# Slot and decay rows by bfloat16 products instead of float32 transposes, in a three-layer mixture-of-experts kernel

## The chip, the cores and the metric

One core of a Trainium2 chip runs the whole program in one launch. The metric is device time in microseconds. Before: median 1460.57 us of 3 runs (1457.16 to 1462.82).

## The reference

256 tokens with 1024 features pass through two layers of a first block and one layer of a second block. All inputs and outputs are float32.

- First block, per layer: a mixer (gated linear attention by chunks and a spatial gating unit), attention to a memory of 256 rows, and a mixture of 16 experts, each followed by a residual and a layer norm.
- Second block: a mixer with causal attention of 8 heads and a state space part (SSD) with 16 heads, a mixture of 16 experts, a gated projection and a last norm.
- Every mixture picks one group of four experts for a token, and two experts in it. An expert computes silu(x Wg) * (x Wu) and multiplies it by Wd; the token's result is the weighted sum over its two experts.
- In the SSD part the decay between tokens l and s of head h is exp(cs[l, h] - cs[s, h]) for s not after l, where cs is the cumulative sum of dt * a over the tokens:

```
decay_to_end = jnp.exp(da_cs[..., -1:] - da_cs)
y_diag = jnp.einsum('bgcls,bgjcls,bcsgjp->bclgjp', cb, decay_in, xdt)
```

## The kernel before

**Projections.** Weights come from HBM in pieces of 1 MB, in an order written out for SyncE's queue. A piece is split into a rounded part (ScalarE) and a rest (VectorE), the tiles `whl`, and three one-pass products stand for one exact one (`proj`, `proj_full`).

**Expert stages.** `moe` runs three times, once a layer. Tokens of an expert are put into 64 slots. `pos` (line 861) holds for each token (partition) and each of the 16 experts the slot, counted from 1, or 0. `Dm` is its one-hot form with tokens on partitions and gathers the tokens of four experts at a time into `XG` (`gather`). The loop at line 1011 takes the experts in eight pairs. For pair i TensorE does, in this order: gate product (`up(i, 0)`), spread of pair i-2 (`spread`), half a gather for the next four experts, up product (`up(i, 1)`), down product of pair i-1 (`down`), the other half gather, in pair 0 the slot gates (`slot_gates`), then `rows(i)`, a fill and `turned(i)`. The two experts of a pair fill 64 columns of the array each, so that their products run in pairs. `rows(i)` (line 969) makes `DT`, the one-hot form with slots on partitions and tokens along the row, by which `spread` brings results back to tokens: a column of `pos`, broadcast to 128 columns, is transposed by TensorE for each expert and each half of the tokens, so that each row of the result holds all tokens' slots; VectorE compares it with the slot's own number (`slot`).

All these TensorE instructions are pinned (`pin`, lines 66 to 75): they keep their order on the engine. Everything that is not pinned is ordered by a planner from modelled times and priorities. The weights of an expert are loaded into whatever buffer comes free (`expert_load`, line 206), in a fixed order; the first 20 pieces of a stage are loaded ahead of it, each later one waits until the products of an earlier piece are done.

**SSD.** `ssd` (line 1166) gets the cumulative sums `cs` from three products of a triangle matrix, then the masked products `cb` of the two groups, and then `heads(h0, n)` runs four heads at a time, between which stand the gate projections (`gates`, line 1317). A head needs its column of `cs` in every row: two transposes of the broadcast column (line 1201) into the PSUM tile `csr`; ScalarE or VectorE subtract the column and form `se`, ScalarE takes the exponential, VectorE multiplies by `dt` and `cb`, and three products (`ssy`) follow. `csr`, `dtp`, the gather's and the products' small PSUM tiles share four buffers (`rp`, line 59).

Of the kernel before, what the change touches and what calls it, by code (L numbers as in the profile page):

```python
# [9 lines left out]
BF16 = mybir.dt.bfloat16  # L10
AF = mybir.ActivationFunctionType
OP = mybir.AluOpType
# [3 lines left out]
T = 256  # L16
# [8 lines left out]
class Net:  # L25
# [94 lines left out]
    def setup1(self):  # L120
        nc, d = self.nc, self.jp
        self.upinc = self.const("upinc", [128, 128])
        self.ones = self.const("ones", [128, 128])
        self.later = self.const("later", [128, 128])
        self.half = self.const("half", [128, 2])
        self.iot = self.const("iot", [128, CAP])
        self.slot = self.const("slot", [128, 1])
        self.tri4 = self.const("tri4", [128, 4, 4])
        nc.vector.memset(self.ones, 1.0)
        self.upb = self.const("upb", [128, 128], BF16)  # L130
        self.ts(self.upb, d, 0.0, None, OP.is_gt)
        self.oneb = self.const("oneb", [128, 128], BF16)
        nc.vector.memset(self.oneb, 1.0)
        self.ts(self.upinc, d, 0.0, None, OP.is_ge)
        self.ts(self.later, d, 0.0, 1.0 / 16.0, OP.is_lt, OP.mult)
        nc.vector.memset(self.later[64:128, 0:64], 0.0)
        nc.vector.memset(self.half, 0.0)
        nc.vector.memset(self.half[0:64, 0:1], 1.0 / 16.0)
        nc.vector.memset(self.half[64:128, 1:2], 1.0 / 16.0)
        self.side = self.const("side", [128, 2])  # L140
        self.ts(self.side, self.half, 16.0, None, OP.mult)
        self.i2 = self.const("i2", [128, 64])
        self.add(self.i2, self.ident[:, 0:64], self.ident[:, 64:128])
        nc.gpsimd.iota(self.iot, pattern=[[1, CAP]], base=1, channel_multiplier=0,
                       allow_small_or_imprecise_dtypes=True)
        if self.cap < CAP:
            nc.vector.memset(self.iot[:, self.cap:], -1.0)
        scr = self.s2("scr", [128, 128])
        self.stt(scr[:, 0:64], self.i2, 1.0, self.iot, OP.mult, OP.mult, accum_out=self.slot)
        e = self.s2("e4", [128, 4, 4])  # L150
        nc.gpsimd.iota(e, pattern=[[-1, 4], [1, 4]], base=0, channel_multiplier=0,
                       allow_small_or_imprecise_dtypes=True)
        self.ts(self.tri4, e, 0.0, -1.0e-37, OP.is_lt, OP.mult)
# [694 lines left out]
    def moe(self, lg, xs, second, finish, gc, route, Wg, Wu, Wd, fill, source):  # L848


        nc = self.nc
# [9 lines left out]
        pos = self.sm("pos", [128, 2, 16], bufs=1)  # L861
        self.stt(pos, pp, 1.0, sel, OP.add, OP.mult)
        Dm = self.t8("Dm", [128, 2, 16, 64], F32R)

        def slots(e, n, tts=slice(0, 2)):
            m = tts.stop - tts.start
# [84 lines left out]
        H, DT, PS = {}, {}, {}  # L951
# [16 lines left out]

        def rows(i):
            with self.urgent("rows"):  # L970
                p = self.rp([128, 2, T], "dtp")
                for s in range(2):
                    for tt in range(2):
                        self.flip(p[:, s, tt * 128:(tt + 1) * 128],
                                  pos[:, tt, 2 * i + s:2 * i + s + 1].to_broadcast([128, 128]))
                DT[i] = self.s2("DT", [128, T], F32R)
                for s in range(2):
                    h = slice(64 * s, 64 * s + 64)
                    self.ts(DT[i][h], p[h, s], self.slot[h], None, OP.is_equal)

        def down(i, apart=False):

# [28 lines left out]
        for i in range(NE // 2):  # L1011
            pg = up(i, 0)
            if i > 1:
                spread(i - 2)
            gather(i // 2 * 4 + 4, (4 * (i % 2),))
            pu = up(i, 1)
            h = middle(pg, pu)
            if i:
                down(i - 1)
            gather(i // 2 * 4 + 4, (4 * (i % 2) + 2,))  # L1020
            if i == 0:
                slot_gates()
            if i == last and over:
                self.tc.keep_in_program_order(
                    nc.vector.tensor_scalar(flag, cm, float(self.cap), None, op0=OP.is_gt))
            rows(i)
            fill(i)
            turned(i, h)
# [137 lines left out]
    def ssd(self, xs, bc, zs, dt):  # L1166

        nc, a = self.nc, self.a
        da = self.sm("da", [128, 2, 16], bufs=1)
        self.stt(da, dt, -1.0, self.hv[:, 1:2, :].to_broadcast([128, 2, 16]), OP.mult, OP.mult)  # L1170
        p = self.rp([128, 2, 16], "csp")
        self.mm(p[:, 0, :], self.upinc, da[:, 0, :], True, True)
        self.mm(p[:, 1, :], self.ones, da[:, 0, :], True, False)
        self.mm(p[:, 1, :], self.upinc, da[:, 1, :], False, True)
        cs = self.sm("cs", [128, 2, 16], bufs=1)
        nc.vector.tensor_copy(cs, p)
        cb = []
        for g in range(2):
            p = self.rp([128, 384], "cbp")
            self.mm(p[:, 0:256], bc[:, g, 0:128], bc[:, 2 + g, :], True, True)  # L1180
            self.mm(p[:, 256:384], bc[:, g, 128:256], bc[:, 2 + g, 128:256], True, True)
            c = self.s2("cb", [128, 3, 128])
            p = p.rearrange("p (a b) -> p a b", a=3)
            self.mul(c[:, 0::2, :], p[:, 0::2, :], self.upinc[:, None, :].to_broadcast([128, 2, 128]))
            self.cp(c[:, 1, :], p[:, 1, :])
            cb.append(c.rearrange("p a b -> p (a b)"))
        u = self.t8("u")
        v = self.vec([a["ssd_norm_g_2"][0]])

        Y = []  # L1190

        def heads(h0, n):

            c = h0 // 8
            if h0 % 8 == 0:
                Y[:] = [self.acc([128, 8, 64], "ssy") for _ in range(2)]
            for h in range(h0, h0 + n):
                with self.urgent("sc"):
                    p = self.rp([128, 256], "csr")
                    for tt in range(2):  # L1200
                        nc.tensor.transpose(p[:, tt * 128:(tt + 1) * 128],
                                            cs[:, tt, h:h + 1].to_broadcast([128, 128]), self.ident)
                with self.urgent("se"):
                    e = self.s2("se", [128, 384])
                    for o, r, k in ((e[:, 0:256], p, cs[:, 0, h:h + 1]),
                                    (e[:, 256:384], p[:, 128:256], cs[:, 1, h:h + 1])):
                        if h % 2:
                            self.ts(o, r, k, 0.0, OP.subtract, OP.min)
                        else:
                            self.act(o, r, AF.Relu, scale=-1.0, bias=k)  # L1210
                    self.act(e, e, AF.Exp, scale=1.0 if h % 2 else -1.0)
                    self.stt(e[:, 0:256], e[:, 0:256], dt[:, 0, h:h + 1], cb[c][:, 0:256], OP.mult, OP.mult)
                    self.stt(e[:, 256:384], e[:, 256:384], dt[:, 1, h:h + 1], cb[c][:, 256:384], OP.mult, OP.mult)
                x0, x1 = (xs[:, i, h * 64:(h + 1) * 64] for i in range(2))
                with self.urgent("sy"):
                    self.mm(Y[0][:, h % 8, :], e[:, 0:128], x0, True, True)
                    self.mm(Y[1][:, h % 8, :], e[:, 128:256], x0, True, False)
                    self.mm(Y[1][:, h % 8, :], e[:, 256:384], x1, False, True)
            if (h0 + n) % 8:
                return  # L1220
            for tt in range(2):
                o = u[:, tt, c * 512:(c + 1) * 512]
                self.mul(o.rearrange("p (h d) -> p h d", h=8),
                         xs[:, tt, c * 512:(c + 1) * 512].rearrange("p (h d) -> p h d", h=8),
                         self.hv[:, 2, 8 * c:8 * c + 8, None].to_broadcast([128, 8, 64]))
                self.add(o, o, Y[tt].rearrange("p h d -> p (h d)"))
                self.mul(o, o, zs[:, tt, c * 512:(c + 1) * 512])
                ss = self.sm("ss", [128, 1])
                sq = self.s2("ssq", [128, 512])
                self.act(sq, o, AF.Square, accum_out=ss)  # L1230
                rs = self.sm("rs", [128, 1])
                self.rsqrt(rs, ss, 1e-6, 1.0 / 512.0)
                self.stt(o, o, rs, v[:, 0, c * 512:(c + 1) * 512], OP.mult, OP.mult)
        return u, heads
# [309 lines left out]
```

## Time and profile before

| | |
|---|---|
| median of 3 runs | 1460.57 us (1457.16 to 1462.82) |
| the profiled execution | 1460.11 us |
| its span | 1458.3 us |
| mean granted TensorE clock | 0.976 of full |
| HBM read | 419.18 MB |

The execution's own time is 1.8 us more than its span. Times in the trace are microseconds from the span's start. PE is TensorE's products, PEld its weight loads, DVE VectorE, ACT ScalarE. Products are pipelined, so that the duration of one is longer than the distance between two starts; float32 products appear as two instructions each, transposes as one. The DMA share is how much of the 16 DMA engines' time their packets fill.

### The profile page before, as it was taken

To read this page: it belongs to the slowest core of one execution; us is meant where nothing else is said; L and a number is where in the kernel's file an instruction comes from. 1 tells how busy PE (TensorE), PEld (TensorE's weight loads), DVE (VectorE), ACT (ScalarE), POOL (GpSimd) and SP (SyncE) were. 2 spreads that over 40 slices of the span, in tenths; PEclk is the share of its full clock that TensorE was granted. 3 is DMA by queue.
4 is the path that set the end of the run, shared out by engine and by line. 5 is a ranking of instruction groups with operands and counts; after the bars stand their busy time and mean duration, and the time that the engine had idled before them with its cause. 6 is when DMAs were issued, how large, how long until landed. Compare 5 with 4: busy or idle time off the path is not lost. (4 is left out here: it accounts for less than half of the span.)

```text
span 1458.3 us, 18050 instructions
## 1 busy us (share of the span) xinstructions
PE 1375.7 (94%) x7258; PEld 899.7 (62%) x7258; DVE 636.3 (44%) x1088; ACT 504.8 (35%) x784; POOL 63.7 (4%) x107
## 2 busy tenths in 40 slices
PE   8999999999988898999899998799999979999987
PEld 7889897444433686898444433499878864444335
DVE  5754754412111767654512111657776641212134
ACT  5634443211101474443211101548764440111132
POOL 2110000000000103000000000000000000000000
PEclk9999999999999999999899999899999989999998
DMA  9745557799999965446799999844534679999991
GB/s 341 271 173 173 174 178 267 280 399 421 420 419 420 320 224 175 145 174 243 297 404 380 422 420 420 326 133 134 185 129 137 227 288 378 421 380 420 420 380 44
DMA packets 101964, 421.50 MB, mean 289 GB/s; under 512 B 10676, under 2 KB 10896, under 8 KB 65008
## 3 DMA queue, kind: packets, MB, share of 16 engines
q1 hardware_dynamic: 97968, 409.17, 72.4%
q0 software_dynamic: 3904, 11.09, 2.3%
q8 instruction: 60, 0.98, 0.3%
q14 instruction: 32, 0.26, 0.0%
HBM read 419.18 MB, written 1.05 MB: 288 GB/s over the span
## 5 line engine op out<-in xcount | busy, mean ns | idle before, releaser
L64 PE MATMUL gu<-we,XG 128*64 128x512 f32 x1536 | 347.0, 596 | 4.2 <-DMA we<-in_w_up_dram 1.9
L78 DVE TENSOR_TENSOR whl<-raw,whl 128x1024 fp32r<-128x1024 f32 (+1 forms) x210 | 241.1, 1163 | 144.6 <-ACT whl L98 143.7
L98 ACT ACTIVATE whl<-raw 128x1024 fp32r<-128x1024 f32 (+1 forms) x210 | 208.2, 1009 | 200.8 <-PE acc L64 97.2
L64 PEld LDWEIGHTS gu<-we,XG 128*64 128x64 f32 x1536 | 108.1, 137 | 208.2 <-issue 193.9
L64 PE MATMUL acc<-whl,xTh 128*128 128x512 f32 (+2 forms) x640 | 193.0, 387 | 4.6 <-ACT xTh L98 3.4
L64 PE MATMUL dn<-we,mid 128*64 128x512 f32 x768 | 179.3, 599 | 16.0 <-DMA we<-in_w_down_dram 13.9
L64 PEld LDWEIGHTS dn<-we,mid 128*64 128x64 f32 x768 | 58.0, 138 | 130.2 <-issue 101.6
L64 PEld LDWEIGHTS acc<-whl,xTh 128*128 128x128 f32 x640 | 119.6, 194 | 29.9 <-ACT xTh L98 4.0
L64 PE MATMUL facc<-xTh,whl 128*128 128x256 f32 x640 | 123.8, 289 | 1.7 <-ACT xTh L98 1.7
L64 PE MATMUL acc<-whl,xTl 128*128 128x512 f32 (+1 forms) x320 | 119.8, 385 | 0.2 <-DVE xTl L78 0.2
L95 ACT ACTIVATE dh<-dn,gsl 128x512 fp32r<-128x512 f32 x42 | 28.9, 688 | 258.8 <-PE dn L64 258.8
L78 DVE TENSOR_TENSOR mid<-mid,gu 128x512 f32<-128x512 f32 x24 | 25.3, 1056 | 211.3 <-PE gu L64 138.7
L64 PEld LDWEIGHTS facc<-xTh,whl 128*128 128x128 f32 x640 | 103.2, 195 | 2.4 <-ACT xTh L98 1.9
L64 PE MATMUL facc<-xTl,whl 128*128 128x256 f32 x320 | 91.6, 287 | 0.0
L87 DVE SCALAR_TENSOR_TENSOR dl<-dn,gsl,dh 128x512 fp32r<-128x512 f32 x42 | 31.5, 750 | 127.6 <-ACT dh L95 125.2
L95 ACT ACTIVATE XG<-gath,gc 128x256 f32<-128x256 f32 x48 | 25.3, 535 | 125.8 <-PE gath L64 117.8
L64 PEld LDWEIGHTS acc<-whl,xTl 128*128 128x128 f32 x320 | 60.5, 193 | 12.7 <-issue 0.7
L64 PEld LDWEIGHTS facc<-xTl,whl 128*128 128x128 f32 x320 | 61.9, 193 | 0.5 <-issue 0.3
L92 DVE TENSOR_SCALAR XG<-gath,gc 128x256 f32<-128x256 f32 x32 | 17.1, 543 | 100.6 <-ACT XG L95 100.2
L95 ACT ACTIVATE mid<-gu 128x512 f32<-128x512 f32 x24 | 14.3, 595 | 121.9 <-PE gu L64 115.4
L64 PE MATMUL acc<-whl,oTh 128*128 128x512 f32 x160 | 49.5, 402 | 0.5 <-ACT oTh L98 0.5
L64 PEld LDWEIGHTS gath<-Dm,xsh 128*128 128x128 f32 x192 | 30.7, 221 | 27.0 <-issue 17.1
(366 smaller groups left out, 1759.3 us busy)
## 6 DMA issues: line engine op xcount, KB each, us to landing
we<-in_w_gate_dram SPq DMA_DIRECT2D x96, 1024.0 KB, 12.7
we<-in_w_up_dram SPq DMA_DIRECT2D x96, 1024.0 KB, 11.8
we<-in_w_down_dram SPq DMA_DIRECT2D x96, 1024.0 KB, 16.7
raw<-in_w_in_dram SPq DMA_DIRECT2D x38, 1024.0 KB, 10.2
raw<-in_w_out_dram SPq DMA_DIRECT2D x12, 1024.0 KB, 5.0
raw<-in_wk_x_dram SPq DMA_DIRECT2D x8, 1024.0 KB, 9.1
raw<-in_wv_x_dram SPq DMA_DIRECT2D x8, 1024.0 KB, 5.7
raw<-in_wq_x_dram SPq DMA_DIRECT2D x8, 1024.0 KB, 5.0
```

Of the source, the lines that this page charges most:

```text
L64: return self.nc.tensor.matmul(out, lhsT=l, rhs=r, start=start, stop=stop, skip_group_check=True)
L78: return self.nc.vector.tensor_tensor(out, a, b, op=op)
L87: return self.nc.vector.scalar_tensor_tensor(out, a, s, b, op0=op0, op1=op1, **k)
L92: return self.nc.vector.tensor_scalar(out, a, s1, s2, op0=op0, op1=op1)
L95: return self.nc.scalar.activation(out, a, f, **k)
L98: return self.nc.scalar.activation(out, a, AF.Copy)
```

## The change

In both places the transposes of a broadcast column are replaced: the 16 columns are turned once into 16 rows in bfloat16, and a product with a broadcast column of the 16x16 identity (`pick`, bfloat16, three times below each other at partitions 0, 32 and 64) copies one row to all rows of the result.

For the experts the turned rows are `posT` (slots are whole numbers up to 256, which bfloat16 holds exactly). They are made once a stage by `slot_rows`, called in pair 0 behind the slot gates: two transposes and a copy. `rows(i)` then has two products with 16 rows and 64 columns each and one comparison on 128 rows.

For the decays the 16 rows are split into three bfloat16 parts that add up to the float32 value, at partitions 0, 32 and 64 of a tile of 96 rows that is zero elsewhere; one product of 96 rows adds the parts again. The split takes two transposes and six VectorE instructions, ahead of the first head. Each head then has one product of 256 columns instead of two transposes.

`i2`, a constant of the setup, becomes a temporary tile.

```diff
+        self.pick = self.const("pick", [96, 16], BF16)
+        nc.vector.memset(self.pick, 0.0)
+        for i in range(3):
+            nc.vector.tensor_copy(self.pick[32 * i:32 * i + 16], self.ident[0:16, 0:16])
...
+        posT = self.sm("turned", [96, T], BF16, bufs=1)[0:16]
+
+        def slot_rows():
+
+            p = self.rp([16, T], "posp")
+            for tt in range(2):
+                self.flip(p[:, tt * 128:(tt + 1) * 128], pos[:, tt, :])
+            nc.vector.tensor_copy(posT, p)
...
-                p = self.rp([128, 2, T], "dtp")
+                p = self.rp([128, T], "dtp")
                 for s in range(2):
-                    for tt in range(2):
-                        self.flip(p[:, s, tt * 128:(tt + 1) * 128],
-                                  pos[:, tt, 2 * i + s:2 * i + s + 1].to_broadcast([128, 128]))
+                    self.mmp(p[64 * s:64 * s + 64], self.pick[0:16, 2 * i + s:2 * i + s + 1].to_broadcast([16, 64]), posT,
+                             True, True)
                 DT[i] = self.s2("DT", [128, T], F32R)
-                for s in range(2):
-                    h = slice(64 * s, 64 * s + 64)
-                    self.ts(DT[i][h], p[h, s], self.slot[h], None, OP.is_equal)
+                self.ts(DT[i], p, self.slot, None, OP.is_equal)
...
             if i == 0:
                 slot_gates()
+                slot_rows()
...
+        rows = self.sm("turned", [96, T], BF16, bufs=1)
+        nc.vector.memset(rows, 0.0)
+        p = self.rp([16, T], "csx")
+        for tt in range(2):
+            nc.tensor.transpose(p[:, tt * 128:(tt + 1) * 128], cs[:, tt, :], self.ident)
+        left = self.s2("csl", [16, T])
+        nc.vector.tensor_copy(rows[0:16], p)
+        self.tt(left, p, rows[0:16], OP.subtract)
+        nc.vector.tensor_copy(rows[32:48], left)
+        nc.vector.tensor_copy(rows[64:80], left)
+        self.tt(left, left, rows[64:80], OP.subtract)
+        nc.vector.tensor_copy(rows[64:80], left)
...
-                    for tt in range(2):
-                        nc.tensor.transpose(p[:, tt * 128:(tt + 1) * 128],
-                                            cs[:, tt, h:h + 1].to_broadcast([128, 128]), self.ident)
+                    self.mm(p, self.pick[:, h:h + 1].to_broadcast([96, 128]), rows, True, True)
```

## Rows read from the trace of the kernel before

**Rows 1.** The page's busy times, shares of the span and instructions by engine.
```profile
PE 1375.7 (94%) x7258; PEld 899.7 (62%) x7258; DVE 636.3 (44%) x1088; ACT 504.8 (35%) x784; POOL 63.7 (4%) x107
```

**Rows 2.** Busy time by stretch: length, PE, PEld, DVE, ACT, POOL, clock, DMA share, GB/s.
```profile
260.00:290.00 30.00, 29.77 (x164) 15.54 (x165) 13.26 (x25) 4.47 (x9) 0.00 (x0) 0.96 0.66 261
...
410.00:470.00 60.00, 52.01 (x229) 19.32 (x228) 6.79 (x11) 5.12 (x9) 1.85 (x3) 1.00 1.01 420
870.00:930.00 60.00, 49.46 (x200) 18.58 (x196) 16.74 (x24) 11.82 (x15) 1.05 (x2) 0.95 1.02 412
1350.00:1400.00 50.00, 46.15 (x204) 17.17 (x202) 5.15 (x7) 4.25 (x7) 0.00 (x0) 1.00 1.02 419
```

**Rows 3.** Who waited for whom: total us, times, longest.
```profile
PE dn L64 <- DMA we<-in_w_down_dram: 13.9, 11, 2.0
```

**Rows 4.** Busy time of short stretches, one in each expert stage.
```profile
287.00:289.00 2.00, 2.00 (x12) 0.72 (x10) 0.00 (x0) 0.00 (x0) 0.00 (x0) 1.00 0.60 156
...
792.00:794.00 2.00, 2.00 (x12) 0.72 (x10) 0.83 (x1) 0.00 (x0) 0.00 (x0) 1.00 0.06 25
...
1285.00:1287.00 2.00, 2.00 (x12) 0.67 (x10) 0.74 (x1) 0.00 (x0) 0.00 (x0) 1.00 0.03 12
```

**Rows 5.** Order of time, TensorE, pair 0 of stage one: start, length, operation, count.
```profile
282.61 0.65 PE L75 MATMUL dtp<-ident,pos 128*128 128x128 f32 x4
283.10 0.60 PE L75 MATMUL gut<-ident,mid 128*128 128x128 f32 x4
283.63 1.08 PE L64 MATMUL gu<-we,XG 128*64 128x512 f32 x4
```

**Rows 6.** The same, pair 1.
```profile
306.73 0.60 PE L75 MATMUL dtp<-ident,pos 128*128 128x128 f32 x4
...
307.16 0.60 PE L75 MATMUL gut<-ident,mid 128*128 128x128 f32 x4
```

**Rows 7.** Order of time, TensorE: one-pass products (first) and two-pass ones.
```profile
16.46 0.39 PE L64 MATMUL facc<-xTh,whl 128*128 128x256 f32 x2
...
525.75 1.13 PE L64 MATMUL pz<-v 17*128 17x256 f32 x4
```

**Rows 8.** Order of time, transpose of 16 columns and its copy, stage one's mixer.
```profile
24.88 0.27 PE L538 MATMUL alp<-ident,kl 128*16 128x128 f32 x1
25.19 0.41 DVE L539 COPY v<-alp 16x256 f32<-16x256 f32 x1 [0.16 <-PE alp L538]
```

**Rows 9.** Order of time, VectorE, pair 0 of stage one.
```profile
283.02 0.17 DVE L78 TENSOR_TENSOR gd<-gd,side 128x16 f32<-128x16 f32 x1
```

**Rows 10.** Order of time, head of the SSD stage; idle before and its releaser in brackets.
```profile
1054.14 0.18 DVE L1176 COPY cs<-csp 128x32 f32<-128x32 f32 x1
...
1054.97 1.23 DVE L78 TENSOR_TENSOR whl<-raw,whl 128x1024 fp32r<-128x1024 f32 x1
...
1055.08 0.82 PE L1201 MATMUL csr<-ident,cs 128*128 128x128 f32 x6
...
1058.91 0.65 PE L1201 MATMUL csr<-ident,cs 128*128 128x128 f32 x4 [1.25 <-ACT cb L98]
...
1059.76 0.48 PE L64 MATMUL acc<-whl,xTh 128*128 128x512 f32 x1
```

**Rows 11.** The same, heads 8 to 15.
```profile
1087.13 1.03 PE L1201 MATMUL csr<-ident,cs 128*128 128x128 f32 x8
...
1089.05 0.40 PE L1201 MATMUL csr<-ident,cs 128*128 128x128 f32 x2 [0.89 <-DVE se L92]
```

**Rows 12.** Groups of VectorE instructions by form: count, busy us, mean ns, idle before.
```profile
L91 DVE TENSOR_SCALAR e<-e,sm 128x256 f32<-128x256 f32 x16 | 4.9, 350 | 0.3
...
L78 DVE TENSOR_TENSOR cb<-cbp,upinc 128x256 f32<-128x256 f32 x2 | 0.8, 421 | 0.3 <-PE cbp L64 0.3
```

**Rows 13.** Order of time, TensorE, before stage three.
```profile
1193.68 0.55 PE L64 MATMUL gath<-Dm,xsh 128*128 128x256 f32 x1 [3.65 <-DVE Dm L78]
```

**Rows 14.** Busy time of the stretch around that wait.
```profile
1188.00:1194.00 6.00, 0.57 (x4) 0.44 (x4) 4.75 (x15) 5.97 (x7) 0.00 (x0) 0.50 1.01 425
```

More of the change, by code (lines that the diff above doesn't have):

```diff
@@ L139, in setup1 @@
         nc.vector.memset(self.half[64:128, 1:2], 1.0 / 16.0)
+        self.pick = self.const("pick", [96, 16], BF16)
+        nc.vector.memset(self.pick, 0.0)
+        for i in range(3):
+            nc.vector.tensor_copy(self.pick[32 * i:32 * i + 16], self.ident[0:16, 0:16])
         self.side = self.const("side", [128, 2])
         self.ts(self.side, self.half, 16.0, None, OP.mult)
-        self.i2 = self.const("i2", [128, 64])
-        self.add(self.i2, self.ident[:, 0:64], self.ident[:, 64:128])
+        i2 = self.s2("i2", [128, 64])
+        self.add(i2, self.ident[:, 0:64], self.ident[:, 64:128])
         nc.gpsimd.iota(self.iot, pattern=[[1, CAP]], base=1, channel_multiplier=0,
@@ L148, in setup1 @@
         scr = self.s2("scr", [128, 128])
-        self.stt(scr[:, 0:64], self.i2, 1.0, self.iot, OP.mult, OP.mult, accum_out=self.slot)
+        self.stt(scr[:, 0:64], i2, 1.0, self.iot, OP.mult, OP.mult, accum_out=self.slot)
         e = self.s2("e4", [128, 4, 4])
```

## The prediction

> **What bounds the kernel now.** I read the page's busy table first, then busy time by stretch, then who waited for whom, then the order of time around the two places that change. TensorE is busy for 94% of the span [rows 1], so at first sight every transpose that goes is time that comes back. The stretches correct this. In the three expert stages the 16 DMA engines are busy all the time (share 1.01 to 1.02, 412 to 420 GB/s) and TensorE, early on busy throughout, has idle time: 8.0 us of the 60 from 410 on, 10.5 of the 60 from 870 on, 3.9 of the 50 from 1350 on [rows 2]. The longest wait of TensorE is of down products for their weights, 13.9 us in 11 pieces [rows 3]. So an expert stage ends when its weights have arrived. What TensorE does sooner or later there counts only where the queue itself waits for TensorE to free a buffer. Such holes are few: one around 287 us in stage one, one at 792 in stage two, one at 1285 in stage three (shares 0.60, 0.06 and 0.03) [rows 4]; the hole near 288 lies in the stretch 260 to 290, whose share is 0.66. Behind the last hole the queue runs full to the end of the stage. The SSD stage, from 1054 on, is the other case: little DMA, TensorE nearly always busy, and at its head a chain from the cumulative decays to the first heads.
>
> **Expert stages, pair by pair.** Removed per pair are four transposes of a broadcast column, in a row from 282.61 to 283.10 in pair 0 and from 306.73 to 307.16 in pair 1, 0.49 and 0.43 us of TensorE [rows 5, 6]. Added are two bfloat16 products of 256 columns, each into 64 output rows. No bfloat16 product of that width is in the trace. Nearest is a one-pass product of 128x256: two of them take 0.39 us with 0.28 for one alone, so 0.12 each [rows 7]. If the two share the array, as the pairs of half-width weight products do, they cost 0.12 together, otherwise 0.24. The upper end is the two-pass float32 product of 17x256, four in 1.13 us, some 0.25 each, so 0.50 for two [rows 7]. I take 0.24, because the one-pass row is nearest: 0.2 less per pair, between 0.3 less and 0.1 more. VectorE makes DT in one 128x256 instruction instead of two on 64 rows, about 0.48 us less per pair; it has time there, and I count nothing.
>
> The new products are 16 rows by 64 columns, between work that uses the whole array. A change of shape is in the trace between the turned gate (128 columns) and the next gate product (64): the four turns begin at 283.10, the last of them 0.33 later by their pace of 0.11, and the product at 283.63, so 0.20 behind it, 0.09 more than the pace [rows 5]. [...]
>
> **The new wait of pair 0.** slot_rows puts two transposes of 16 columns, a VectorE copy and only then rows(0) into TensorE's written-out order, and behind rows(0) stand the turned gate of pair 0 and the whole of pair 1. Nothing that is not pinned fills the hole. The same operation exists for the gate's low-rank input: transpose at 24.88, copy of 16x256 from 25.19, 0.41 us long [rows 8], so 0.72 us from the start of the transpose to the end of the copy. Here: transposes at 282.61 and 282.73, copy ended at 283.45 if VectorE is free (its multiplication for the slot gates ends at 283.19 [rows 9]; with the reduction behind it ahead of the copy as well, some tenths later), products 0.24, and the turned gate at 283.7 to 284.0 where it was 283.10. I take 0.7 us late, bounds 0.4 and 1.1, once per stage.
>
> What reaches the end: stage one's hole is freed by pair 1's first product and so carries the 0.7 alone; in stages two and three the hole comes in pair 3, behind two more rows() that each win 0.2, so 0.3 each. Behind the last weights there is one more rows(7) in stages one and three, worth 0.2 each; stage two ends waiting for its weights. Sum of the three: 0.7 + 0.3 + 0.3 - 0.4 = 0.9 us later. Bounds: 0.4 late and 0.3 won in each later rows() give +0.1, -0.2 and -0.5, -0.6 in all; 1.1 late and 0.1 lost in each of the six give +3.9.
>
> **The SSD stage.** Removed are 32 transposes at about 0.11 us (six in 0.82, one alone 0.27) [rows 10], 3.5 us; added 16 products at 0.12 and two transposes, 2.2 us. TensorE does 1.3 us less. But all 32 sit where TensorE waits for others: 16 between 1055.08 and 1059.56, where a wait of 1.25 us stands between them, and 16 from 1087 on, where a wait of 0.89 follows the first eight [rows 10, 11]; there PSUM buffers, freed by VectorE and ScalarE, set the pace. I count 0.3 of the 1.3.
>
> Ahead of the first product comes a new chain: two transposes, then six VectorE instructions on 16x256, each for the one before or its tile: copy from PSUM 0.41, subtract from PSUM 0.42, two copies at 0.35, subtract 0.42, copy 0.35 (durations of the nearest forms [rows 8, 12]), 2.3 us, with the transposes 2.8. The memset of the 96 rows needs nothing and lies earlier. The decays are ready at 1054.32 and the first transpose ran at 1055.08 [rows 10]; with the chain it is 1057.1, so 2.0 late. Behind it stand on TensorE, as now ordered, all of heads 0 to 3 and then the gate product (the first is issued at 1059.76 and its weights are split by 1056.20 [rows 10]), so the planner has work that it could put ahead. I take half, 1.0 late; bounds 0 (all covered) and 4.0 (the 1.23 us weight split that stood behind the copy of the decays, and the masks, come into the middle of the chain). Sum of the stage 0.7, bounds -1.3 and +4.
>
> **The rest.** The setup has a memset and three copies of 16 columns more on VectorE, while it waits for the first x; i2 becomes a temporary. Nothing.
>
> The sum: 0.9 + 0.7 = 1.6 us on the profiled execution's 1460.11 (span 1458.3 and 1.8 around it), so **1461.7**; the median shown, 1460.57, is 0.5 above that execution, and I name 1462.0. The bounds give 1458.2 to 1468.0.
>
> **Rivals.**
> *TensorE is the bound after all.* It is busy without a gap for the first four pairs or so of each stage. Then each of 24 pairs gives back 0.46 (the mean of the two rows) - 0.12 = 0.34, 8.2 us, less three times 0.7 in pair 0, and the SSD stage its 1.3: 7.4 less, 1453. Against it: the full DMA share and the waits for weights [rows 2, 3], which come back longer by what TensorE wins. Chance 0.10.
> *The SSD chain stalls TensorE and the clock falls; slower.* If the six instructions stand between two weight splits (2 x 1.23) and both masks (2 x 0.42), the first product comes at 1060.4, 5.3 us late, and if the gate product still stands behind it, TensorE idles that long in one piece. [...] With the 0.9 of the expert stages that is 9.2, 1469. [...] Chance 0.10.
> *The planner orders unrelated work anew.* Everything but the expert loops is ordered from modelled times, and a few instructions more can change who goes first in all three mixers. That moves some 5 us either way, a wait like that of 3.65 us [rows 13] more or less and its clock: 1456 or 1467. Chance 0.12, a quarter of it each way past the bound below.
> *The change does what it says but nothing of it reaches the end:* 1460 to 1461, part of the forecast.
>
> **How the numbers follow.** The forecast, a small loss of 0 to 5 us or so, has 0.68, its own range 1458 to 1467. A measurement of this kernel tells about 0.5%, 7.3 us, from no change. Faster by more: 0.10 from the first rival and 0.03 from the third, 0.13. Slower by more: 0.10 and 0.03, 0.13. Within: 0.74. The range reaches to both rivals, 1453 to 1469.
>
> **What would show it.** Right: stages with the DMA share at 1.0 and longer waits of down products; a TensorE wait of 0.5 to 1 us for VectorE in pair 0 of each stage; the hole of stage one ending some 0.7 us later; products of rows() at 0.12 or in pairs; the first head's row product 1 to 2 us further behind the copy of the decays; 24 DT instructions of 0.48. Wrong: stages shorter by 2 us or more, a half-clock stretch near 1055, mixers of stages one or two that differ by several us.

## The result and the profile after

The changed kernel takes 1476.05 us, median of 4 runs (1473.05 to 1477.52), against 1460.07 (1457.16 to 1462.82) for the kernel before in the same comparison: a ratio of 1.0101, 95% interval 1.0087 to 1.0116, 16.0 us slower. The forecast was 1462.0 with a range up to 1469, and the chance of slower by over 0.5% was put at 0.13. The prediction was wrong.

The page of the kernel after: span, then busy time by engine.

```profile
span 1475.7 us, 17911 instructions
...
PE 1385.0 (94%) x7202; PEld 898.7 (61%) x7202; DVE 626.3 (42%) x1078; ACT 505.4 (34%) x784; POOL 64.0 (4%) x107
```

TensorE has 56 products fewer than in [rows 1] and is busy 9.3 us longer; 17.4 us came onto the span. Where they lie is found by setting the start of each instruction against that of the same instruction before:

| place in the kernel after | later by (us) |
|---|---|
| ahead of pair 0 of stage one (by 270) | +0.3 |
| pair 0 of stage one (282 to 292) | +2.2, all of it come back by 488, 1.9 near 426: 0.0 |
| behind the overflow test, end of stage one (488 to 495) | +4.4 |
| pair 0 of stage two (729 to 735) | +2.3 |
| head of the SSD stage (1058 to 1075) | +6.3 |
| heads 8 to 15 (1100 to 1109) | +2.0 |
| wait before stage three (near 1200) | +1.0 |
| pair 0 of stage three (1234 to 1240) | +2.4 |
| small steps in between, and the rest of stage three | -1.3 |

Six stretches of these places, busy time by engine, granted clock, DMA share, GB/s:

```profile
284.00:288.00 4.00, 4.00 (x16) 1.70 (x16) 0.53 (x2) 0.60 (x1) 0.00 (x0) 0.61 0.92 383
492.00:495.00 3.00, 3.00 (x9) 2.35 (x8) 1.65 (x4) 0.00 (x0) 0.00 (x0) 0.50 0.85 315
731.00:734.00 3.00, 3.00 (x10) 0.87 (x10) 0.10 (x1) 0.60 (x1) 0.00 (x0) 0.50 1.00 421
1065.00:1075.00 10.00, 7.46 (x22) 5.22 (x23) 4.63 (x14) 4.40 (x9) 0.00 (x0) 0.52 0.26 101
1102.00:1109.00 7.00, 5.70 (x19) 4.14 (x19) 5.27 (x14) 4.03 (x12) 0.00 (x0) 0.56 0.43 150
1236.00:1239.00 3.00, 3.00 (x9) 0.94 (x10) 0.00 (x0) 0.60 (x1) 0.00 (x0) 0.50 0.98 407
```

The same work in the kernel before:

```profile
283.00:287.00 4.00, 4.00 (x23) 1.66 (x23) 1.21 (x4) 0.60 (x1) 0.00 (x0) 1.00 1.02 426
487.60:490.60 3.00, 3.00 (x14) 2.44 (x13) 3.00 (x5) 0.00 (x0) 0.00 (x0) 1.00 1.01 350
726.00:729.00 3.00, 3.00 (x15) 1.06 (x16) 0.75 (x3) 0.60 (x1) 0.00 (x0) 1.00 1.02 429
1058.00:1068.00 10.00, 9.09 (x54) 7.96 (x55) 5.18 (x14) 5.87 (x15) 0.00 (x0) 1.00 0.26 102
1088.00:1095.00 7.00, 5.05 (x29) 3.63 (x28) 6.12 (x16) 4.89 (x13) 0.00 (x0) 1.00 0.55 197
1218.50:1221.50 3.00, 3.00 (x19) 1.35 (x18) 1.21 (x4) 0.60 (x1) 0.00 (x0) 1.00 1.01 423
```

The third column from the end is the point: in all six the granted clock is 0.50 to 0.61, so 0.50 for all or most of the stretch ("half clock" below), where the kernel before had 1.00. Elsewhere the stages keep their character: in the expert stages the DMA share is as in [rows 2] and the waits for down weights as in [rows 3] (15.0 us in 12 pieces).

Pair 0 of stage one, order of time, TensorE (to be set beside [rows 5]), and behind "..." pair 1 (beside [rows 6]):

```profile
282.93 0.39 PE L75 MATMUL posp<-ident,pos 128*16 128x128 f32 x2
283.82 0.42 PE L64 MATMUL dtp<-turned,pick 16*64 16x256 bf16 x2 [0.50 <-DVE turned L875]
284.17 1.11 PE L75 MATMUL gut<-ident,mid 128*128 128x128 f32 x4
285.21 5.00 PE L64 MATMUL gu<-we,XG 128*64 128x512 f32 x18
...
308.76 0.64 PE L64 MATMUL gath<-Dm,xsl 128*128 128x256 f32 x4
309.33 0.29 PE L64 MATMUL dtp<-turned,pick 16*64 16x256 bf16 x2
309.55 0.65 PE L75 MATMUL gut<-ident,mid 128*128 128x128 f32 x4
310.14 1.08 PE L64 MATMUL gu<-we,XG 128*64 128x512 f32 x4
```

The wait is there, 0.50 us; the turned gate starts 1.07 after [rows 5], 0.31 of it inherited, so 0.76 by this edit. But the four turns now take until 285.21, 1.04 us where they took 0.53: the granted clock is 0.50 from 284 to 286, where the kernel before had 1.00 from 283 to 285.

The end of stage one: an output product behind the branch of the overflow test; in brackets what it waited for ("issue": nothing that the profile shows), called the issue wait below.

```profile
487.85 0.40 PE L64 MATMUL acc<-whl,mTh 128*128 128x512 f32 x1
490.81 0.50 PE L64 MATMUL acc<-whl,mTh 128*128 128x512 f32 x1 [2.56 <-issue]
```

The head of the SSD stage (to be set beside [rows 10]), TensorE and then VectorE:

```profile
1061.20 0.39 PE L1191 MATMUL csx<-ident,cs 128*16 128x128 f32 x2 [0.54 <-DVE cs L1186]
1065.60 1.03 PE L64 MATMUL csr<-turned,pick 96*128 96x256 bf16 x4 [2.70 <-DVE turned L1198]
...
1069.80 1.12 PE L64 MATMUL ssy<-xs,se 128*128 128x64 f32 x4 [1.74 <-DVE se L87]
```

```profile
1060.96 0.18 DVE L1186 COPY cs<-csp 128x32 f32<-128x32 f32 x1
1061.63 0.41 DVE L1193 CAST turned<-csx 16x256 bf16<-16x256 f32 x1 [0.48 <-PE csx L1191]
1061.97 1.20 DVE L78 TENSOR_TENSOR whl<-raw,whl 128x1024 fp32r<-128x1024 f32 x1
1063.10 0.41 DVE L78 TENSOR_TENSOR csl<-csx,turned 16x256 f32<-16x256 f32 x1
1063.43 0.73 DVE L78 TENSOR_TENSOR cb<-cbp,upinc 128x256 f32<-128x256 f32 x2
...
1065.26 0.28 DVE L1198 CAST turned<-csl 16x256 bf16<-16x256 f32 x1
```

From the end of the copy of the decays to the first row product it is 4.46 us, where [rows 10] have 0.76: 3.7 late. The six small instructions are as cheap as foretold (0.28 to 0.41), but a weight split and the masks stand between them, and the planner put nothing of TensorE's into the wait.

### The profile page after: what moved, and what is told of

Read it like the earlier page. It is cut to its first block, busy times and chain, and to the rows that moved or that the text cites. A ratio compares the mean times of both kernels' runs of the same rounds, so it can differ in the third digit from the quotient of the medians.

```text
span 1475.7 us, 17911 instructions
## 1 busy us (share of the span) xinstructions
PE 1385.0 (94%) x7202; PEld 898.7 (61%) x7202; DVE 626.3 (42%) x1078; ACT 505.4 (34%) x784; POOL 64.0 (4%) x107
## 5 line engine op out<-in xcount | busy, mean ns | idle before, releaser
L64 PE MATMUL gu<-we,XG 128*64 128x512 f32 x1536 | 350.8, 601 | 2.9 <-DMA we<-in_w_gate_dram 2.3
L64 PE MATMUL acc<-whl,xTh 128*128 128x512 f32 (+2 forms) x640 | 196.5, 392 | 4.3 <-ACT xTh L98 3.4
```

Source lines behind the costliest of these rows:

```text
L64: return self.nc.tensor.matmul(out, lhsT=l, rhs=r, start=start, stop=stop, skip_group_check=True)
```

## Experiments

At the start, for e1 to e4, I held that the clock falls behind the new waits, in pair 0 as at the SSD head. When e3 and e4 spoke against that for pair 0, three theories took its place. S: in pair 0 TensorE's work became shorter and thinner, and the clock falls for that, with or without the wait. P: the issue wait comes with the place of TensorE's instructions. C: the SSD head loses by the uncovered chain and the clock behind it. The rival to all three is that any new order of work draws some half-clock stretches. Each ratio below is to the kernel before as run beside that experiment, with its 95% interval.

**The two parts alone.** e1 keeps only the SSD part of the change, e2 only the expert part.

```diff
@@ e1 against the changed kernel; rows(i) as before @@
-                slot_rows()
@@ e2 against the changed kernel; the chain of the decays goes too @@
-                    self.mm(p, self.pick[:, h:h + 1].to_broadcast([96, 128]), rows, True, True)
+                    for tt in range(2):
+                        nc.tensor.transpose(...)
```

> The SSD part of the change alone; the expert stages keep their transposes. Theory (clock): in the changed kernel the SSD stage loses 6.3 us at its head, where a wait of 2.7 us and half-clock stretches of 10.2 us follow the split chain, and 2.0 us at heads 8 to 15, where another half-clock stretch of 6.8 us begins; alone it should cost 7 to 9 us, 1467 to 1469, with both stretches in the trace and none behind pair 0 of the expert stages. Rival (the planner's new order of unrelated work, or where the code lies, makes the loss): the cost is not tied to the part, 1460 or 1474, and shows in other stages. Rival (chain alone): the head costs the 3.7 us by which the first row product was late, 1464.

> The expert part alone; the SSD stage keeps its transposes. Theory (clock): each stage's pair 0 loses 0.6 us to the wait for the copied rows and 1.7 us more to a half-clock stretch of 3.4 us that begins there; stages two and three carry it to the end, stage one gives it back against its weights, so about 5 us, 1465; if the wait of 2.6 us at the end of stage one, for which no releaser is seen, belongs to this part, 1469. Rival (wait alone, my prediction): 0.9 us, 1461.

e1: 1465.98, ratio 1.0034 (1.0021 to 1.0047). e2: 1468.21, 1.0043 (1.0031 to 1.0056). By the ratios each loses, 5.0 and 6.3 us; together that is 11.3, where the whole change loses 14.7. The issue wait is in e2 (3.0 us) and not in e1; the loss at the SSD head is in e1 (+6.2) and not in e2.

**Pair 0.** Three edits of e2, so with the expert part alone: e3 makes the rows of slots early, so that nothing waits for them; e4 puts the turned gate of pair 0 ahead of its rows; e6 leaves pair 0 its transposes and makes the rows of slots behind the turned gate. In all three the old call of slot_rows goes, and in e4 the turned gate of pair 0 at its old place (not shown).

```diff
@@ e3 against e2 @@
             pg = up(i, 0)
+            if not i:
+                slot_rows()
@@ e4 against e2 @@
+            if not i:
+                slot_rows()
+                turned(i, h)
             rows(i)
@@ e6 against e2 @@
-            rows(i)
+            rows(i) if i else rows0(i)     # rows0: the transposes of before
             fill(i)
             turned(i, h)
+            if not i:
+                slot_rows()
```

> The expert part with slot_rows right behind the first gate product, so that its copy is done some 15 us before rows(0) asks for it. Theory (clock): without the wait pair 0 does not fall to half clock, and the part costs nothing or gains up to 1 us, 1459 to 1461. Rival (the clock falls because transposes of whole columns were replaced by shorter work behind the 16 small slot gate products, not because of the wait): half clock remains in pair 0, 1464.

> The expert part with slot_rows where the change has it, but in pair 0 the four transposes of the gate come between slot_rows and rows(0) and fill the wait. Theory (clock falls after the wait): no half clock in pair 0, and as e3 within 1 us, 1459 to 1461. Rival (it falls because less is done there): half clock remains, 1464.

> The expert part of the change alone, with pair 0's rows by transposes as before and slot_rows behind the turned gate of pair 0. Theory S (pair 0 loses because TensorE's work there becomes shorter and thinner, and its clock falls; the wait only adds to that): no half clock and no loss in pair 0 of the three stages, and what is left of the expert part's loss is the issue wait at the end of stage one (+4.4) and the later clock stretches: 1464 to 1465. Rival (the shorter rows cost the clock elsewhere as soon as pair 0 doesn't): half clock moves to pair 1 or 2 and the time stays at 1467 to 1468.

e3: 1467.04, 1.0037 (1.0018 to 1.0057). e4: 1464.06, 1.0016 (1.0007 to 1.0025). e6: 1465.97, 1.0026 (1.0015 to 1.0038). Busy time from 282 to 292 in e3, and then in e6:

```profile
282.00:292.00 10.00, 10.00 (x54) 5.26 (x55) 2.53 (x6) 1.64 (x3) 0.00 (x0) 0.83 0.79 310
```

```profile
282.00:292.00 10.00, 10.00 (x59) 4.97 (x59) 2.75 (x8) 0.97 (x2) 0.00 (x0) 1.00 0.89 343
```

In e3 the profile has TensorE busy for all of the 10 us, without a wait, and still the clock fell, in pair 0 of stages one and two (+1.6 each); so the wait isn't needed. In e6, with the longer rows in pair 0 alone, it stays at 1.00 in pair 0 of all three stages, and does not move to a later pair. e4, with the turns between the transposes and the rows, has it in stage two only (0.85 from 727 to 737). The profiles of all twenty kernels say the same: with the new rows in pair 0 (the change, e2, e3, e4, e10, e16) the clock falls there in 13 of 18 stages, with the transposes in none of 42. So S holds for pair 0, as a cause that acts in most stages, not in all (in stage three only together with the SSD part: 2 of 2, else 0 of 4). Whether it is the shorter time or the thinner products, no run separates.

**The issue wait.** e5 is the kernel before with slot_rows (and the constant pick) added, its rows unused. e9 is e6 with twelve more row products in pair 5 of each stage, e10 is e2 with fourteen, e13 is e6 with eighteen, e16 the changed kernel with twenty-two; they repeat a product into the same place.

```diff
@@ e5, against the kernel before @@
             turned(i, h)
+            if not i:
+                slot_rows()
@@ e9 against e6; e10, e13 and e16 alike with 8, 10 and 12 @@
-                    self.mmp(p[64 * s:64 * s + 64], ..., posT, True, True)
+                    for _ in range(7 if i == 5 else 1):
+                        self.mmp(p[64 * s:64 * s + 64], ..., posT, True, True)
```

> The kernel before, with slot_rows' two transposes and its copy behind the turned gate of pair 0 in each expert stage, their result unused; rows() as before. Theory P (the issue wait of TensorE of 2.6 to 3.0 us at the end of stage one, which all kernels with the new expert part showed and no other, comes with the place of its instructions, here moved by two): that wait of 2.6 us shows here too, with a stretch of half clock behind it, +4.4 us, 1465; no half clock in pair 0, since TensorE's rows there are as long as before. Rival (it comes with the new products themselves): no issue wait at the end of stage one, 1461 to 1462.

> The expert part with pair 0's rows by transposes, and twelve more products of the row of pair 5 in each stage (their result the same), so that TensorE has as many instructions ahead of the branch of the overflow test as in the kernel before: a transpose is a weight load and a product, two rows, a pair of new products is four rows where four transposes were eight, so the expert part alone takes 24 rows out of a stage. Theory P (the issue wait at the end of stage one comes with the place of TensorE's instructions there): no issue wait behind that branch, no half clock behind it, 1461 to 1462, about the kernel before. Rival (it comes with the new products, or with the branch being reached sooner): a wait of 2.6 to 3.4 us for issue as in all kernels with the new expert part, 1465 to 1466.

> The expert part as changed (new rows in pair 0 too, with the wait), with fourteen more products of the row of pair 5 in each stage, which give back the 28 instruction rows that the part takes out. Theories P and S: no issue wait at the end of stage one, but half clock in pair 0 of two stages or three, +2.2 each, of which stage one gives its own back: 1463 to 1465, some 4 below the expert part alone (1468.2). Rival (position doesn't matter): issue wait again, 1468.

> The expert part with pair 0's rows by transposes and eighteen more row products in pair 5 of each stage, some 5072 TensorE records ahead of the branch at the end of stage one. Theory P (place of the instructions): no issue wait there in any execution, 1460 to 1463, one group of times. Rival (the new products or the pace bring it, and the padded kernels escape it by chance): most executions near 1467, as with twelve products.

> The changed kernel with twenty-two more row products in pair 5 of each stage and nothing else, some 5075 TensorE records ahead of the branch. Theory P: no issue wait at the end of stage one, and 4 to 5 us less than the changed kernel: 1471 to 1472, with the losses of pair 0 and of the SSD head as they were. Rival: 1475 to 1477.

The rows of TensorE (products, then weight loads, in brackets) up to the branch, in the kernels before, after, e9 and e13:

```profile
0.00:486.50 486.50, 463.75 (x2508) 308.09 (x2508) 204.92 (x348) 163.71 (x248) 28.55 (x47) 0.99 0.79 304
```

```profile
0.00:486.70 486.70, 465.53 (x2494) 308.05 (x2494) 200.77 (x345) 163.81 (x248) 28.55 (x47) 0.98 0.79 303
```

```profile
0.00:483.60 483.60, 464.49 (x2508) 307.91 (x2508) 201.30 (x346) 163.75 (x248) 28.51 (x47) 0.99 0.80 305
```

```profile
0.00:483.50 483.50, 463.35 (x2514) 306.81 (x2514) 201.29 (x346) 163.41 (x248) 28.52 (x47) 0.99 0.80 305
```

Loads and products together: 4988 in the changed kernel, 28 fewer than before. All five kernels with 4988 or 4992 (after, e2, e3, e4, e6) have the issue wait, 2.6 to 3.4 us. Before, e5 (5020), e13 (5028) and e16 (5032) don't. e9 and e10 stand at the 5016 of the kernel before, with three or four fewer of TensorE's other rows (waits, branches; 5059 and 5058 rows of all kinds against 5062): e10 came 4.7 us late to the first product behind the branch in its profile (a wait of 5.57 us, where e9 and e6 have 0.87), and e9's executions fall in two groups, 1460.0 and 1461.3, and ten from 1466.9 to 1471.4. The one that was profiled is of the first group and has no issue wait; that the ten have it is not shown. By their medians e5 takes 1462.35 (1.0006, 0.9996 to 1.0016), e9 1467.86 (1.0048, 1.0034 to 1.0063), e10 1471.47 (1.0055, 1.0033 to 1.0076), e13 1460.09 (1.0000, 0.9988 to 1.0013). So two expectations failed. e5 should have had the wait if any shift brought it, and a few instructions more did not. And padding to exactly the old count did not free e10 of it, nor, by its times, e9; by what they missed the theory became sharper. P holds as: too few instructions ahead of the branch, with a boundary within some four of where the kernel before stood. The moment at which the branch is reached does not decide: e4 is there at 481.5 and has the wait, e9's profile at 481.4 and e17 at 481.5 have none. e16 is the changed kernel with that alone mended: 1471.93 (1.0062, 1.0044 to 1.0079, where the change has 1.0101), no issue wait, as P expected. The instruction queue shows what differs. Its row between 478 and 484, in the kernel before:

```profile
q8 instruction: 1, 0.02, 1.1%
```

In the same stretch of the changed kernel that queue moves nothing; its next packet starts at 488.2, about when TensorE begins to wait. So it is in all the profiles: in the six with the wait (the change, e2, e3, e4, e6, e10) no packet of q8 starts in the 28 us ahead of the branch and the next comes 3.7 to 4.4 us behind it; in the fourteen without it one starts 1.9 to 3.8 us ahead. In the changed kernel these packets start at 455.77 and 488.23 and the branch at 484.49; in the kernel before one starts at 480.52 and the branch at 484.25. Each takes 1.0 to 1.1 us; on the page q8 has 60 packets and 0.98 MB, before as after. The one from 488.23 fits the stall, which ends at 490.81; whether the branch was taken, and which packet held what TensorE waited for, the trace doesn't show. That an edit of 28 instructions goes with whether a packet comes ahead of an untouched branch is what these runs show; by what mechanism, they don't.

**The SSD head.** e12 keeps only the first bfloat16 part, one copy in place of six instructions. e11 marks the chain urgent. e7 asks for the first gate product ahead of the first heads; e8 does so in the kernel before. e14 makes heads 0 to 3 by transposes as before and runs the chain behind them, for heads 4 to 15.

```diff
@@ e12 against e1; the five instructions on left go too @@
-        left = self.s2("csl", [16, T])
@@ e11 against e1, around da, cs and the chain @@
+        with self.tc.high_priority():
@@ e7 against e1, e8 against the kernel before @@
-        for w in [0, -1, 4, -1, 8, -1, 12, -1]:
+        for w in [-1, 0, 4, -1, 8, -1, 12, -1]:
@@ e14 against e1; under h < 4 the two transposes of before @@
+                    if h < 4:
...
+                    else:
                         self.mm(p, self.pick[:, h:h + 1].to_broadcast([96, 128]), rows, True, True)
...
+            if not h0:
+                decay_rows()
```

> The SSD part alone, with the first gate product asked for ahead of heads 0 to 3 in the code. Theory C (the whole loss at the head of the SSD stage, 6.2 us in the SSD part alone, is the uncovered chain and the half clock behind it): the gate product fills the chain, no half clock near 1057, the head of the stage loses 0 to 2 us: 1460 to 1462. Rival (the loss is a clock lottery that any new order draws): half clock at the head all the same, or as much of it a little later, 1465 to 1467.

> The kernel before with the first gate product asked for ahead of heads 0 to 3: the control for the order alone. Theory C: 1459 to 1462, about no change, so that what the other kernel wins against the SSD part alone is the covered chain. Rival (the order by itself is worth several us): 1455 or 1465.

> The SSD part alone with the decays' chain marked urgent for the planner: VectorE's order has one weight split and the two masks between its steps, as without the mark, but the first product of decays is asked for a little sooner, and two large products stand between it and the chain's transposes. Theory C (the loss at the head is the length of TensorE's wait and the half clock behind it): the wait at the head stays near 2 to 2.7 us and the loss with it, 1465 to 1466; if it falls below 1 us, no half clock there and 1461 to 1462. Rival (not the wait): half clock at the head whatever the wait.

> The SSD part with only the first bfloat16 part of the decays, one copy in place of six instructions (it leaves out the two low parts, so the decays are coarser). Theory C: VectorE's chain is 1.9 to 3.6 us shorter, TensorE's wait at the head 0 to 0.8 us, no half clock there; the head of the stage is 1 us before or behind that of the kernel before: 1460 to 1462. Rival (the short 96-row products with their thin stretch bring the clock down, not the chain): half clock at the head as before, 1465 to 1466.

> The SSD part, with the rows of heads 0 to 3 by transposes as before and the new chain behind their subtractions, for heads 4 to 15 alone. Theory C (the head loses by TensorE's wait for the chain, and by the clock that falls behind it): no wait for the chain, no half clock at the head, the stage within 1 us of the kernel before: 1460 to 1462. Rival (the short products of the heads themselves cost the clock): half clock near 1057 or in heads 4 to 15 as much as in the SSD part alone, 1464 to 1466.

e12: 1463.34, 1.0011 (0.9997 to 1.0025); its row products, TensorE:

```profile
1051.36 0.38 PE L64 MATMUL csr<-turned,pick 96*128 96x256 bf16 x2
1052.45 0.44 PE L64 MATMUL csr<-turned,pick 96*128 96x256 bf16 x2 [0.71 <-ACT se L95]
1054.62 0.38 PE L64 MATMUL csr<-turned,pick 96*128 96x256 bf16 x2 [1.73 <-ACT cb L98]
```

With the short chain no product waits for it, and the head loses 2.1 us where it lost 6.2. A half-clock stretch of 3.4 us is left there (mean clock 0.94 from 1050 to 1080), against what I expected, where e1 has 10.2 us (0.83). e11: 1466.16, 1.0038 (1.0027 to 1.0049): the planner's mark left one weight split in the chain, the wait stayed at 2.9 us and the loss with it. e7 and e8 take the same time, 1466.04 (1.0027, 1.0018 to 1.0036) and 1466.08 (1.0025, 1.0013 to 1.0036): with the gate product in front the SSD part costs nothing, but that order costs 4 us by itself, against what I expected of the control; there the first heads come later and a row product of e7 waits 1.9 us for VectorE. e14: 1461.85, 1.0005 (0.9993 to 1.0017). Its head, order of time, and busy time from 1050 to 1080 there and in the changed kernel:

```profile
1052.78 0.82 PE L1221 MATMUL csr<-ident,cs 128*128 128x128 f32 x6
...
1054.61 0.39 PE L1187 MATMUL csx<-ident,cs 128*16 128x128 f32 x2 [0.19 <-ACT se L95]
```

```profile
1050.00:1080.00 30.00, 27.45 (x142) 22.36 (x141) 21.50 (x44) 17.33 (x30) 0.00 (x0) 1.00 0.39 137
```

```profile
1050.00:1080.00 30.00, 24.82 (x117) 19.79 (x116) 16.90 (x40) 16.62 (x30) 0.00 (x0) 0.83 0.32 106
```

The same chain, computed in full behind work that covers it, costs the head nothing. C holds for the larger part of the loss. e14 also gives the first four heads their transposes back, so that of the 6.2 up to the 2.1 left in e12 may come from the new row products rather than from the chain.

**All together.** e15 is the change with the mends of e13 and e14. e17 gives heads 8 to 15 their transposes back as well; e18 gives each of their products twice.

```diff
@@ e17 against e15 @@
-                    if h < 4:
+                    if h < 4 or h > 7:
@@ e18 against e15 @@
+                        for _ in range(2 if h > 7 else 1):
                             self.mm(p, self.pick[:, h:h + 1].to_broadcast([96, 128]), rows, True, True)
```

> The whole change with the three mends: pair 0 and heads 0 to 3 by transposes, eighteen more row products in pair 5. If the three causes are all: 1460 to 1463, no difference from the kernel before. Rival (the parts draw each other's clock stretches, as the whole change lost 14.7 us where its parts lost 11.3): 1466 or more. Faster than before by more than 2 us is expected by neither.

> The change with its three mends and with the rows of heads 8 to 15 by transposes as well (the new products are left in pairs 1 to 7 and heads 4 to 7). Theory S: no half clock near 1091, 1460 to 1462, no difference from the kernel before. Rival (the rest of the loss lies elsewhere, or moves on): 1464 or more.

> The change with its three mends, where each row product of heads 8 to 15 is given twice in a row (the same result). Theory S (TensorE's work there became shorter, so it waits longer for VectorE and ScalarE, and the clock falls): waits near 3 to 4 us in place of 4.7, half clock shorter or gone, 1461 to 1463. Rival (the 96-row bfloat16 product itself, of whatever length): half clock near 1091 as in mixed, 1465 to 1466.

e15: 1465.57, 1.0027 (1.0015 to 1.0040): not 1460 to 1463. No issue wait, no half clock in the pairs 0 or at the head (1.00 there); its profile is 4.4 us longer than that of before, and 4.5 lie in heads 8 to 15 (1.0 more before stage three and 1.1 less behind it cancel). Two more runs were made on the thought that their shorter work costs the clock, and both said no: e17 1466.23 (1.0039, 1.0021 to 1.0057), e18 1465.01 (1.0024, 1.0013 to 1.0034). The waits of TensorE from 1080 to 1102 in e17, with transposes as before:

```profile
PE ssy L64 <- DVE se L87: 1.5, 1, 1.5
PE csr L1242 <- DVE se L92: 1.2, 2, 1.0
```

The first is 0.3 in the kernel before. In e14, e15, e17 and e18 the row products of heads 4 to 7 stand behind the first gate product (1073.04 in e17), so VectorE's subtractions for heads 4 to 7 come 8.5 us later (1074.06 in e17, 1065.54 before), and its work on these heads meets the subtractions of heads 8 to 15. That is argued from the order; no run took it apart. And the waits alone do not decide it: e2, whose SSD code is that of before, has the waits of [rows 11] there to 0.02 us and loses 2.8 us to half clock at 1096 (0.86 from 1084 to 1108), the kernel before doesn't (1.00). It is not chance of an execution alone: of the nine profiles whose SSD code is as before, the four with new rows in pair 0 (e2, e3, e4, e10) have this stretch and the five without (before, e5, e6, e9, e13) don't. Why one falls and the other not stays open, as does why e14 alone came out at 1461.9 with the same stretch in its profile (it was 2.3 us ahead of the kernel before when it got there).

## Why the prediction was wrong, step by step

*Expert stages, pair by pair.* The costs were small, as foretold, and so was the gain: from the second half of the gather to the gate product it is 1.38 us in pair 1 against 1.44 [rows 6], so 0.06 won, not 0.2. The two ends of the 1.44, in the kernel before:

```profile
306.25 0.63 PE L64 MATMUL gath<-Dm,xsl 128*128 128x256 f32 x4
...
307.69 0.65 PE L64 MATMUL gu<-we,XG 128*64 128x512 f32 x2
```

From the start of the two products to that of the next operation it is 0.22, as taken; but they begin 0.57 behind the gather where transposes began 0.48 behind it. The 0.09 more is the 0.09 of [rows 5], at another change of shape, for which my sum had nothing; what takes it isn't shown.

*The new wait of pair 0.* Its size was right: 0.50 us of wait, 0.76 late. **What failed is that the step ended there.** The clock was priced only for a long idle piece in the SSD stage; here it fell behind a wait of half a microsecond, and in e3 behind none, with the new rows as the cause that e6 shows. That took another 1.4 to 1.7 us in each stage. "What reaches the end", 0.3 in each of the later stages, was 2.3 and 2.4: a loss in pair 0 is not won back by seven pairs at 0.06. In stage one, where I let the whole loss reach the end, it came back: the wait of 1.90 us for weights at 426.86 in the kernel before is gone.

*The SSD stage.* This is the largest term: I took "half, 1.0 late; bounds 0 and 4.0" and the sum 0.7; it was 3.7 late and 6.3 lost. My own upper bound described what happened, weight split and masks in the middle of the chain. The failed step is "so the planner has work that it could put ahead": that it could was in the rows, that it would was not, and [rows 10] showed the opposite, a wait of 1.25 with nothing put into it.

*The rival of the falling clock* had the right outcome, half clock at the SSD head, and the wrong point: I had put it at an idle piece of about 4 us, an estimate of mine from the one wait that the rows have, 3.65 us with 0.50 around it [rows 13, 14]. Here TensorE waited 2.70 us and then 1.74, and the granted clock was 0.52 from 1065 to 1075. Its 9.2 hold 5.3 for the late product, 0.9 for the expert stages and 3 for the clock, half of 6 us at half clock; no run shows that 3 as such: the product came 3.7 late, the head has 10.2 us at half clock and loses 6.3 in all. It had 0.10, and even its 1469 is 7 short, since it held neither the clock in the pairs 0 nor the issue wait.

*What I put at nothing:* the issue wait, 2.6 us and 4.4 with its clock, at a branch that the change doesn't touch. The count of 28 instructions was there to be had from the diff; a reason to fear it wasn't in the rows that I read.

*What held:* TensorE is not the bound of the expert stages (the rival at 1453 is out: 56 products fewer and nothing faster); DT in one instruction of 0.48, 24 times; the mixers of stages one and two take as long as before (0.3 us late at 270; 4.6 at 500, 4.4 at 725).

With its causes mended the expert part alone costs nothing (e13, 1.0000) and the SSD part alone 0.0005 (e14); together they still cost 0.0027 (e15). So at its best the change wins nothing here, and no version beat the kernel before. Of the whole loss, the 2.0 at heads 8 to 15 and the 1.0 ahead of stage three, which e1 has and e2 doesn't, stay unexplained. The prediction's own range stands there twice, as 1458.2 to 1468.0 and as 1458 to 1467; the sums give the first.

## What to carry to other kernels

When a change shortens TensorE's work next to a wait, or puts a chain ahead of it, price the clock behind it too: here the places with waits of 0.5, 2.6 and 2.7 us lost 2.2, 4.4 and 6.3, and the first of them lost 1.6 without its wait (e3). New chains go behind the first work that can do without them, as in e14 and e6. And when only a few instructions come or go ahead of a branch, compare what is issued behind the branch before blaming the edit itself.

## What the hardware showed

- In e3, pair 0 of stage one, the granted clock was 0.50 from 286 to 288 (mean 0.83 from 282 to 292) while the profile shows no idle time of TensorE: busy 2.00 of 2 us, and 10.00 of 10.
- Taking 28 TensorE instructions out ahead of a branch brought an issue wait of 2.6 us behind it; with eighteen needless products more a kernel went from 1.0026 of the time before to 1.0000 (e6 to e13). The wait goes with the instruction queue: no packet in the last 28 us ahead of the branch in six profiles with it, one in the last 3.8 us in fourteen without. At the boundary itself one kernel (e9) has executions in two groups, some 7 us apart.
- The same waits to 0.02 us were followed by half clock in one kernel (e2) and not in the other (before), so that a stretch's own waits did not decide its clock.
